# Weaving the mixers of the first half: other step counts behind the matmuls of a hybrid decoder trunk

## The chip, the cores and the metric

The kernel runs on one core of a Trainium2 chip. The metric is device time in microseconds (us). A chip run is repeated, and one execution is taken with the hardware profiler on.

## The reference

Two layers work on x of 1024 rows (tokens) by 1024 columns, in float32. Each layer normalises its input and projects it into three groups of mixers, whose outputs are joined and projected back; then follows a gated MLP with a short causal convolution.

```python
proj = rms_norm(x) @ w_in[layer]
dq, dk, dv, lq, lk, lv, z, xbc, dt = jnp.split(proj, IN_OFFSETS, axis=-1)
o_diff = diff_attention(rope(dq), rope(dk), dv, ...)      # 4 heads, two softmaxes each, causal
o_dil = dilated_attention(rope(lq), rope(lk), lv)         # 6 heads, three sliding windows merged
o_ssd = ssd_mixer(z, xbc, dt, conv_w, ...)                # conv, silu, scan over chunks of 128
x = x + rms_norm(concat(o_diff, o_dil, o_ssd) @ w_out[layer])
g, val = jnp.split(causal_dwconv(rms_norm(x) @ ffn_up[layer]), 2, axis=-1)
x = x + rms_norm((silu(g) * val) @ ffn_down[layer])
```

## The kernel before

Each layer is worked off in two halves T = 0 and 1 of 512 tokens. A product in float32 is made of three matmuls of rounded parts: high by high, high by low and low by high. ScalarE rounds a weight tile (line 144), VectorE subtracts to get the low part (line 145); there are four tiles of each part and three raw ones.

The program is one long list, written out by Python generators, of dense units (matmuls of the projections) and mixer steps. A scheduler of the framework turns the list into one fixed order for every engine, each queue in order. `weave(dense, mixer, counts)` (line 229) takes one dense unit after another, and behind each hangs as many mixer steps as `counts` says. `marks` holds certain matmuls of the unit, every sixth in a block of 24. Step x of n is written with high priority, and its TensorE instructions are ordered behind mark (x + 1) * len(marks) // n - 1, counted from 0. The gate holds TensorE alone; the step's work on other engines is free to go as its data come.

In a layer's first half the order is this. The unit kinds are: six rotary units of dilated heads (`DILC`), four of differential heads (`DIFC`), and seven convolution units (`SSDC`). An `mm3` block (line 216) is 24 matmuls of 512 columns for one half. `DILC` runs alone for T = 0. The first weave has `DIFC` for T = 0 (one block a unit) and `SSDC` for both halves (two blocks a unit). The second weave has `DILC` and `DIFC` for T = 1 (ten units of a block) and four units of the token-major projection `tm_in(1)`, of 24 matmuls of 384 columns each. The third weave has the first three output units `out_units(0)`. After it the rest of both is run out, and the MLP follows, with the heads of T = 1 woven into it.

The mixer list of T = 0 is: 30 steps of three pairs of dilated heads, 22 of two pairs of differential heads, one step that loads five finished head tiles and splits them (`out_load`, line 778), 16 of four state-space chunks: 69. A head pair has eight softmax steps (four blocks of queries, two heads). In `attn` (line 657) step z makes scores (line 610) and softmax (612 to 615; 733 to 735 for the differential pairs, 727 and 728 for the dilated ones) of item z, transposes item z - 1 (750, 751), and multiplies item z - 2 with the values (760). Six steps at the end of each generator drain it; some of them do nothing. `load_head` (line 618) brings queries and keys of the next pair in when the present one is in its last block of queries; of query tiles there are four, which two differential heads fill.

In `ssd` (line 480) a chunk has three steps. The first transposes and scales the inputs and makes the decay matrix (lines 520 to 544); VectorE multiplies it at line 546. The second adds the carried state's part (555 to 560). The third first calls `finish` (line 489, transposes at 492) for the chunk before, then multiplies (566), sums and gates (568, 569), updates the state (572 to 580), and normalises (585, `rstd` at 108 with POOL's power at 114, 589). One step stands ahead of the first chunk, three behind the last, of which the third is its `finish`.

A convolution block is evacuated by `conv` (line 370) with three long VectorE instructions at line 374, then a tanh and a product (391, 392), into scratch tiles of the tag cv, of which there are four, and written to DRAM (393). A rotary block takes two or four products (402, 403, 408 to 411), two roundings (415) and two subtractions on POOL (417). PSUM holds three accumulators. All DMAs are issued by the one queue of SP.

Of the kernel before, what the change touches and what calls it, by code (L numbers as in the profile page):

```python
# [69 lines left out]
def body(ctx, tc, x_in, win, wva, wvb, wvz, wout, wup, wdn, cst, gains, dtb, alog, lamp, kst, rope, out):  # L70
# [158 lines left out]
    def weave(dense, mixer, counts):  # L229
        for n in counts:  # L230
            marks.clear()
            next(dense, None)
            for x in range(n):
                gate = marks[(x + 1) * len(marks) // n - 1]
                with tc.high_priority(), tc.issue_after(gate.ins):
                    next(mixer, None)

    def act_pair():
        return (sp.tile([P, KT, H], F32R, tag="act", bufs=4, name="ah"),
                sp.tile([P, KT, H], F32R, tag="act", bufs=4, name="al"))  # L240
# [68 lines left out]
    def run(*gens):  # L309
        for g in gens:  # L310
            for _ in g:
                pass

    for l in range(NL):
# [113 lines left out]
        def in_unit(name, Ts):  # L428
            hi, lo = wsplit(win[l, IN_IDX[name]])
            for T in Ts:  # L430
                a = acc()
                mm3(a, hi, lo, rhs_of(hT[T]), KT)
                in_evac(name, T, a)
# [38 lines left out]
        def dt_steps(T):  # L472
            dt_chain(T)
            yield
            dt_sums(T)
            yield
# [301 lines left out]
        def out_load(T, pair, ks):  # L778
            for k in ks:
                m = t2("cv", 4)  # L780
                Y.dma_start(m[:], MT[k][T][:] if k < 5 else MS[T][:, k - 5])
                out_split(pair, k, m[:])
            yield

        def tm_in(T, before=None):
            def evac(c, t, a):
                v = t2("cv", 4)
                c0, n = ((0, 384), (384, 256), (640, 384))[c]
                v, a, d = v[:, :n], a[:, :n], a[:, n:n + 6]
                if c < 2:  # L790
                    A.activation(v, a, AF.Copy)
                else:
                    A.activation(v, a, AF.Tanh, scale=0.5)
                    V.scalar_tensor_tensor(v, v, 1.0, a, op0=ALU.add, op1=ALU.mult)
                Y.dma_start(VZ[T][t, :, c0:c0 + n], v)
                if c == 1:
                    e = slice(t * 6, t * 6 + 6)
                    V.tensor_tensor(dtr[T][:, e], d, sm[:, e], op=ALU.add)
                    if t == 3 and T == 0:
                        dt_chain(0)  # L800
            return tm_units([wva[l], wvb[l], wvz[l]], 0, KT, rhs_of(hT[T]), evac, before, pairs=0 if before else 1)

        def out_units(T, pair):
            xs = []
            g1 = load_gain(l, 1)
            g2 = load_gain(l, 2)
            rr = [None] * 4
            sq = [None] * 4

            def evac(c, t, a):  # L810
                if c == 0:
                    rr[t] = rows()
                    sq[t] = tiny()
                A.activation(rr[t][:, c * H:(c + 1) * H], a[:], AF.Copy)
                A.activation(a[:], a[:], AF.Square, accum_out=sq[t][:, c:c + 1])
                if c == 0 and t == 3:
                    xs.extend(load_x(T))
                if c == 1:
                    V.tensor_tensor(sq[t][:, 0:1], sq[t][:, 0:1], sq[t][:, 1:2], op=ALU.add)
                    norm_add(4 * T + t, xs[t], rr[t][:], sq[t], rr[t], g1, False, g2)  # L820
            return tm_units([wout[l, c] for c in range(2)], 0, KT, rhs_of(pair), evac, pairs=1 if T else 0), rr
# [27 lines left out]
        def down_group(T, gi, fT):  # L849
            k0, n = GROUPS[gi]  # L850
            last = gi == len(GROUPS) - 1
            f = [fT[:, 2 * t:2 * t + 2].rearrange("p k n -> p (k n)") for t in range(4)]
            if last and T:
                xs = load_x(T)
                g3 = load_gain(l, 3)
                g0 = load_gain(l + 1, 0) if l < NL - 1 else None

            def evac(c, t, a):
                d = slice(c * H, (c + 1) * H)
                if gi == 0:  # L860
                    A.activation(f[t][:, d], a[:], AF.Copy)
                else:
                    V.tensor_tensor(f[t][:, d], a[:], f[t][:, d], op=ALU.add)  # L863
                if last and T and l == NL - 1:
                    if c == 0:
                        fin.append((rows(), tiny()))
                    r, sq = fin[-1]
                    A.activation(r[:, d], f[t][:, d], AF.Square, accum_out=sq[:, c:c + 1])
                    if c == 1:
                        V.tensor_tensor(sq[:, 0:1], sq[:, 0:1], sq[:, 1:2], op=ALU.add)  # L870
                        rs = rstd(sq[:, 0:1], 1, 1.0 / DM, EPS)
                        for d in (slice(0, H), slice(H, DM)):
                            V.scalar_tensor_tensor(r[:, d], f[t][:, d], rs[:, 0:1], g3[:, d], op0=ALU.mult, op1=ALU.mult)
                            E = G if d.start == 0 else V
                            E.tensor_tensor(r[:, d], xs[t][:, d], r[:, d], op=ALU.add)
                            Y.dma_start(out[4 * T + t, :, d], r[:, d])
                elif last and T and c == 1:
                    fin.append(fin_norm(4 * T + t, xs[t], f[t], g3, g0))
            return tm_units([wdn[l, c] for c in range(2)], k0, n, [gt[k0 + k] for k in range(n)], evac, inner=last and T == 1)
# [18 lines left out]
        def ffn(T, pair, fT):  # L898
            for gi, (k0, n) in enumerate(GROUPS):
                for j in range(k0, k0 + n):  # L900
                    yield from up_pair(T, j, pair)
                if gi < len(GROUPS) - 2:
                    yield from down_group(T, gi, fT)

        SSDC = IN_ORDER[:7]
        DILC = IN_ORDER[7:13]
        DIFC = IN_ORDER[13:]

        def units(names, Ts):
            for n in names:  # L910
                in_unit(n, Ts)
                yield

        NG = len(GROUPS)
        if l == 0:
# [16 lines left out]
            dense = tm_in(0, before)  # L932
# [18 lines left out]
        else:  # L951
            cs, sw, fw, sm, nA, nlam = layer_constants()
            hT[0] = nextT
            dense = tm_in(0)
# [2 lines left out]
        dt_sums(0)  # L957
        run(units(DILC, (0,)))
        mix0 = chain(attn(0, DILH), attn(0, DIFH))
        weave(chain(units(DIFC, (0,)), units(SSDC, (0, 1))), mix0, [2] * 4 + [4] * 7)  # L960
        pair = act_pair()
        mix0 = chain(mix0, out_load(0, pair, range(5)), ssd(0, pair))
        tm1 = tm_in(1)
        weave(chain(units(DILC + DIFC, (1,)), tm1), mix0, [2] * 14)
        mix1 = chain(attn(1, DILH + DIFH), dt_steps(1), ssd(1))
        dense, rs = out_units(0, pair)
        weave(dense, mix0, [3] * 3)
        run(mix0)
        run(dense)
        hold[0] = lastmm[0]  # L970
# [18 lines left out]
        dense, rs = out_units(1, pair)  # L989
        run(dense)  # L990
        hold[0] = lastmm[0]
        dense = down_group(0, NG - 1, fT0)
# [4 lines left out]
        dense = ffn(1, hp, fT1)  # L997
# [8 lines left out]
        dense = down_group(1, NG - 2, fT1)  # L1006
# [89 lines left out]
```

## Time and profile before

| what | us |
|---|---|
| median of 3 runs | 2672.4 (2667.95 to 2674.1) |
| the profiled execution's own time | 2669.15 |
| its span, first to last instruction | 2667.4 |
| TensorE busy (matmuls) | 2605.3 |
| TensorE weight loads | 2163.8 |
| VectorE busy | 1832.6 |
| ScalarE busy | 1247.7 |
| GpSimd (POOL) busy | 230.3 |
| mean granted TensorE clock | 0.995 |

PE is TensorE's matmuls, PEld its weight loads, DVE VectorE, ACT ScalarE, POOL GpSimd, SP the queue that issues DMAs. Busy time is the union of an engine's instructions. An arrow in brackets behind an instruction says how long its engine had been idle before it and what ended that. The clock is granted at 2.4 GHz (1.00) or 1.2 GHz (0.50).

### The profile page before, as it was taken

Reading aid. Unit: us, or ns where it says so; the run is one execution under the profiler, and the core shown is the slowest. Engines: PE = TensorE matmul, PEld = TensorE weight load, DVE = VectorE, ACT = ScalarE, POOL = GpSimd, SP = SyncE. Lnnn points to the kernel's source line nnn. Section 1 sums busy time; section 2 is a strip of 40 time slices with the busy share of each in tenths; the row PEclk is TensorE's granted clock in tenths of the full one; section 3 lists DMA queues with packets and bytes.
Section 4 is the critical chain, followed back from the end, with each engine's and each line's share of the span. In section 5 each row is a group of like instructions: output and inputs, shape, how many; then the busy total and the mean of one; then the engine's idle time right before and its main releaser. Section 6 shows DMA issues by size and latency. Waiting matters only on the chain.

```text
span 2667.4 us, 37072 instructions
## 1 busy us (share of the span) xinstructions
PE 2605.3 (98%) x13448; PEld 2163.8 (81%) x13448; DVE 1832.6 (69%) x3854; ACT 1247.7 (47%) x2179; POOL 230.3 (9%) x228
## 2 busy tenths in 40 slices
PE   7999999999999999999999999999999999999998
PEld 6887788888788877888888878788877888788886
DVE  5567856567877586666765688565688775956666
ACT  4465444555544454333444654455565344543332
POOL 0100210110002010000002012101100110100001
PEclk9999999999999999999999999999999999999999
DMA  6654635344434454333347546454444334633332
GB/s 227 202 185 146 206 121 186 111 119 115 123 101 128 125 187 155 97 95 95 91 161 232 167 142 203 139 161 115 121 115 139 94 111 133 231 97 95 95 99 67
DMA packets 163718, 368.90 MB, mean 138 GB/s; under 512 B 18256, under 2 KB 64208, under 8 KB 163536
## 3 DMA queue, kind: packets, MB, share of 16 engines
q1 hardware_dynamic: 163536, 366.54, 44.1%
q8 instruction: 106, 1.74, 0.3%
q14 instruction: 76, 0.62, 0.1%
HBM read 306.18 MB, written 60.29 MB: 137 GB/s over the span
## 4 chain that ended last, share of the span: by engine, by line
PE 81%; DVE 9%; ACT 3%; DMA 3%; issue 3%; POOL 1%; SPq 0%; ACTq 0%; DVEq 0%; POOLq 0%
PE acc L220 16%; PE acc L223 15%; PE acc L224 15%; PE acc L168 7%; PE acc L164 7%; PE acc L167 7%; PE po L760 4%; PE s L610 3%; PE tr L750 3%; DVE wl L145 1%; POOL rs_r L114 1%; ACT wh L144 1%; DVE P L287 1%; DVE t L288 1%; DMA cv<-MT 1%
## 5 line engine op out<-in xcount | busy, mean ns | idle before, releaser
L220 PE MATMUL acc<-ah,wh 128*128 128x512 f32 x1952 | 775.4, 398 | 0.5 <-ACT ah L271 0.5
L224 PE MATMUL acc<-ah,wl 128*128 128x512 f32 x1952 | 764.8, 392 | 0.0
L223 PE MATMUL acc<-al,wh 128*128 128x512 f32 x1952 | 764.4, 392 | 0.2 <-DVE al L272 0.2
L145 DVE TENSOR_TENSOR wl<-wr,wh 128x1024 fp32r<-128x1024 f32 (+3 forms) x406 | 477.9, 1183 | 274.9 <-ACT wh L144 271.1
L144 ACT ACTIVATE wh<-wr 128x1024 fp32r<-128x1024 f32 (+3 forms) x406 | 406.2, 1007 | 470.0 <-PE acc L223 269.1
L220 PEld LDWEIGHTS acc<-ah,wh 128*128 128x128 f32 x1952 | 366.6, 188 | 80.5 <-issue 9.3
L224 PEld LDWEIGHTS acc<-ah,wl 128*128 128x128 f32 x1952 | 366.6, 188 | 78.1 <-issue 2.4
L223 PEld LDWEIGHTS acc<-al,wh 128*128 128x128 f32 x1952 | 366.9, 188 | 71.7 <-DVE al L272 1.0
L374 DVE SCALAR_TENSOR_TENSOR cv<-acc,cs,cv 128x511 f32<-128x511 f32 (+2 forms) x436 | 324.6, 744 | 17.7 <-ACT cv L372 15.8
L164 PE MATMUL acc<-wh,g 128*128 128x512 f32 x704 | 281.0, 400 | 4.5 <-DVE fT L863 2.2
L167 PE MATMUL acc<-wl,g 128*128 128x512 f32 x704 | 276.5, 393 | 3.0 <-DVE wl L145 3.0
L168 PE MATMUL acc<-wh,g 128*128 128x512 f32 x704 | 275.8, 394 | 0.9 <-DVE g L843 0.9
L164 PE MATMUL acc<-wh,ah 128*128 128x512 f32 (+2 forms) x640 | 225.4, 356 | 10.0 <-ACT wh L144 6.7
L167 PE MATMUL acc<-wl,ah 128*128 128x512 f32 (+2 forms) x640 | 226.3, 354 | 5.8 <-DVE wl L145 5.1
L168 PE MATMUL acc<-wh,al 128*128 128x512 f32 (+2 forms) x640 | 225.1, 353 | 4.3 <-DVE al L272 4.1
L615 ACT ACTIVATE P<-P,tiny 128x128 f32<-128x128 f32 (+7 forms) x224 | 172.9, 773 | 115.1 <-DVE tiny L614 110.4
L612 DVE CUSTOM_DVE_ANT_0 P<-s,kc 128x512 f32<-128x512 f32 (+3 forms) x224 | 129.7, 588 | 108.6 <-PE s L610 107.2
L114 POOL TENSOR_TENSOR rs_r<-rs_m,kc 128x1 f32<-128x1 f32 (+2 forms) x88 | 71.4, 815 | 1398.4 <-DVE rs L115 1256.6
L164 PEld LDWEIGHTS acc<-wh,g 128*128 128x128 f32 x704 | 132.8, 189 | 39.2 <-ACT g L842 3.8
L372 ACT ACTIVATE cv<-acc,cs 128x512 f32<-128x512 f32 x204 | 155.7, 763 | 13.8 <-PE acc L224 13.3
L168 PEld LDWEIGHTS acc<-wh,g 128*128 128x128 f32 x704 | 132.6, 188 | 31.9 <-DVE g L843 4.4
L167 PEld LDWEIGHTS acc<-wl,g 128*128 128x128 f32 x704 | 133.0, 189 | 29.6 <-DVE wl L145 3.8
(173 smaller groups left out, 3138.2 us busy)
## 6 DMA issues: line engine op xcount, KB each, us to landing
wr<-in_wup SPq DMA_DIRECT2D x176, 512.0 KB, 3.6
wr<-in_wdn SPq DMA_DIRECT2D x80, 512.0 KB, 3.5
wr<-in_win SPq DMA_DIRECT2D x54, 512.0 KB, 5.1
wr<-in_wout SPq DMA_DIRECT2D x32, 512.0 KB, 4.4
xd<-t SPq DMA_DIRECT2D x24, 512.0 KB, 2.9
t<-xd SPq DMA_DIRECT2D x24, 512.0 KB, 3.7
t<-in_x SPq DMA_DIRECT2D x16, 512.0 KB, 4.7
Q<-DQ SPq DMA_DIRECT2D x128, 64.0 KB, 2.1
```

What stands on the lines that cost most here:

```text
L144: A.activation(h, r, AF.Copy)
L145: V.tensor_tensor(part(lo), r, fr(h), op=ALU.subtract)
L164: i = T_.matmul(a, xh, hi[:, w], start=(n0 + k == 0), stop=False)
L167: T_.matmul(a, xh, lo[:, w], start=False, stop=False)
L168: lastmm[0] = T_.matmul(a, xl, hi[:, w], start=False, stop=(n0 + k == n - 1))
L220: i = T_.matmul(a[:], hi[:, w], xh, start=(k == 0), stop=False)
L223: T_.matmul(a[:], hi[:, w], xl, start=False, stop=False)
L224: i = T_.matmul(a[:], lo[:, w], xh, start=False, stop=(k == nk - 1))
L372: A.activation(u[:], a[:], AF.Identity, scale=w[:, n:n + 1], bias=w[:, taps:taps + 1])
L374: V.scalar_tensor_tensor(u[:, d:], a[:, :H - d], w[:, n - d:n - d + 1], u[:, d:], op0=ALU.mult, op1=ALU.add)
L612: V.tensor_tensor_reduce(p[:, c:c + n], s[:, :n], mask[:, o:o + n], 1.0, -1e30 if c == 0 else mx[:, e], ALU.add, ALU.max, mx[:, e])
L615: A.activation(p[:, :nk * P], p[:, :nk * P], AF.Exp, scale=scale, bias=nm[:, e], accum_out=den[:, e])
```

## The change

Three lists of counts are changed, the same way in both layers. The number of mixer steps, their content and their order among themselves stay.

```diff
-        weave(chain(units(DIFC, (0,)), units(SSDC, (0, 1))), mix0, [2] * 4 + [4] * 7)
+        weave(chain(units(DIFC, (0,)), units(SSDC, (0, 1))), mix0, [3] * 4 + [5] * 7)
         pair = act_pair()
         mix0 = chain(mix0, out_load(0, pair, range(5)), ssd(0, pair))
         tm1 = tm_in(1)
-        weave(chain(units(DILC + DIFC, (1,)), tm1), mix0, [2] * 14)
+        weave(chain(units(DILC + DIFC, (1,)), tm1), mix0, [2] * 5 + [1] * 9)
         mix1 = chain(attn(1, DILH + DIFH), dt_steps(1), ssd(1))
         dense, rs = out_units(0, pair)
-        weave(dense, mix0, [3] * 3)
+        weave(dense, mix0, [2] * 3)
```

## Rows read from the trace of the kernel before

**Rows 1.** The page: busy time by engine, and the chain that ended last.
```profile
PE 2605.3 (98%) x13448; PEld 2163.8 (81%) x13448; DVE 1832.6 (69%) x3854; ACT 1247.7 (47%) x2179; POOL 230.3 (9%) x228
...
PE 81%; DVE 9%; ACT 3%; DMA 3%; issue 3%; POOL 1%; SPq 0%; ACTq 0%; DVEq 0%; POOLq 0%
```

**Rows 2.** Busy time by stretch, layer 0: stretch, length, each engine (instructions), clock, DMA.
```profile
core 0: us, PE busy (x) PEld busy (x) DVE busy (x) ACT busy (x) POOL busy (x), PEclk, DMA share, GB/s
76.29:109.04 32.75, 32.75 (x146) 27.12 (x146) 17.07 (x22) 8.94 (x12) 5.48 (x4) 1.00 0.72 238
109.04:237.00 127.96, 127.51 (x691) 103.14 (x689) 85.75 (x247) 76.29 (x168) 8.29 (x6) 1.00 0.56 173
237.00:311.50 74.50, 74.41 (x393) 58.37 (x392) 62.10 (x168) 39.05 (x86) 15.39 (x11) 1.00 0.60 194
311.50:346.00 34.50, 31.75 (x189) 29.93 (x188) 29.24 (x51) 15.02 (x39) 11.82 (x11) 0.95 0.52 166
346.00:372.00 26.00, 24.59 (x123) 19.77 (x122) 10.27 (x29) 11.91 (x33) 5.00 (x5) 1.00 0.40 136
```

**Rows 3.** Busy time by stretch, the chunks of layer 1.
```profile
1632.00:1666.00 34.00, 32.08 (x192) 30.45 (x190) 29.09 (x51) 15.08 (x38) 12.07 (x11) 0.95 0.55 174
1666.00:1692.00 26.00, 24.55 (x123) 19.80 (x122) 10.77 (x29) 11.99 (x34) 5.00 (x5) 1.00 0.42 141
```

**Rows 4.** Instructions in order of time, TensorE, 300 to 345: start, us, what.
```profile
314.54 1.55 PE L566 MATMUL tr<-xdt,P 128*128 128x64 f32 x12 [0.68 <-DVE P L546]
...
327.39 0.78 PE L492 MATMUL tr<-kc,yq 128*128 128x128 f32 x3 [1.51 <-ACT yq L589]
...
332.66 0.53 PE L164 MATMUL acc<-wh,ah 128*128 128x384 f32 x1
...
333.76 0.33 PE L167 MATMUL acc<-wl,ah 128*128 128x384 f32 x1
```

**Rows 5.** Instructions in order of time, TensorE, 345 to 380.
```profile
361.10 0.33 PE L492 MATMUL tr<-kc,yq 128*128 128x128 f32 x1 [0.89 <-ACT yq L589]
```

**Rows 6.** Lines 568 and 589, 300 to 372: duration ns min/median/max, first and last start.
```profile
L568 DVE TENSOR_TENSOR y<-tr,y x4: 541/550/557, 317.3 to 355.0; 128x384 f32<-128x384 f32 x4
...
L589 ACT ACTIVATE yq<-y,rs_r x8: 438/454/465, 326.9 to 361.0; 128x192 f32<-128x192 f32 x8
```

**Rows 7.** Busy time 198.21 to 311.50, VectorE, lines 612, 614, 733, 734, 735 singly.
```profile
198.21:311.50 113.29, 14.80 (x64) 1.00 0.54 171
...
198.21:311.50 113.29, 4.64 (x33) 1.00 0.54 171
...
198.21:311.50 113.29, 2.51 (x16) 1.00 0.54 171
...
198.21:311.50 113.29, 3.42 (x16) 1.00 0.54 171
...
198.21:311.50 113.29, 8.65 (x16) 1.00 0.54 171
```

**Rows 8.** Busy time by stretch, the fifth and the seventh convolution unit of layer 0.
```profile
198.21:211.01 12.80, 12.80 (x70) 10.29 (x69) 6.89 (x15) 4.78 (x10) 0.00 (x0) 1.00 0.61 170
222.97:237.00 14.03, 14.03 (x74) 11.19 (x74) 12.96 (x51) 9.07 (x27) 0.00 (x0) 1.00 0.25 78
```

**Rows 9.** Instructions in order of time, TensorE, 216 to 223: a head's scores, its transpose.
```profile
219.18 0.33 PE L610 MATMUL s<-k,Q 128*128 128x128 f32 x2
...
222.91 0.30 PE L750 MATMUL tr<-kc,P 128*128 128x128 f32 x1 [0.45 <-DVE P L735]
```

**Rows 10.** Instructions in order of time, SP's DMA issues, 180 to 262.
```profile
241.52 8.70 SPq L646 DMA_DIRECT2D Q<-DQ  x15
```

**Rows 11.** Instructions in order of time, POOL (268 to 300), then VectorE (270 to 281).
```profile
272.80 3.73 POOL L417 TENSOR_TENSOR g<-g 128x512 fp32r<-128x512 f32 x2 [8.03 <-issue]
...
273.13 2.24 DVE L145 TENSOR_TENSOR wl<-wr,wh 128x1024 fp32r<-128x1024 f32 x1
...
276.76 1.21 DVE L145 TENSOR_TENSOR wl<-wr,wh 128x1024 fp32r<-128x1024 f32 x1
```

**Rows 12.** Busy time of one stretch in the MLP of layer 0.
```profile
992.00:1024.00 32.00, 31.96 (x142) 26.12 (x140) 30.21 (x60) 17.89 (x26) 2.61 (x4) 1.00 0.53 167
```

## The prediction

> **What bounds the kernel now.** I read the page's first section before anything else: TensorE has a matmul in flight for 98% of the span, and the chain of work that ended last runs through it for 81% [rows 1]. So only two things can shorten the program: TensorE idle time inside the changed stages, and time in which its clock was granted at half rate. The second view is busy time by stretch. Of layer 0 it shows the six undisturbed blocks of 24 matmuls ahead of the weave (32.75 us, so 5.46 us a block), the first weave (109.04 to 237.00), ten rotary units (to 311.50), and the two stretches in which the state-space chunks run (311.50 to 346.00 and 346.00 to 372.00) [rows 2]. The reader is to see that the first weave and the rotary units lose 0.45 and 0.09 us, while the chunks lose 2.75 and 1.41 us and have a mean granted clock of 0.95 in the former stretch. Layer 1 repeats it: 1.92 and 1.45 us idle, clock 0.95 [rows 3]. The third view, the matmuls in order of time, names the waits: the diagonal product (line 566) waits 0.68 us for VectorE's line 546, and the transposes of a normalised chunk (line 492) 1.51 us for ScalarE's line 589; soon after, a 384-column matmul takes 0.53 us where 0.33 is usual, which is the granted clock at 1.2 instead of 2.4 GHz [rows 4]; line 492 waits again, 0.89 us, in the output units [rows 5].
>
> **What the change removes.** No instruction is added or removed, DMAs included: the same 69 mixer steps (52 of the heads, one that loads finished heads, 16 of the chunks) are hung behind other matmuls. Before, the first weave takes 8 + 28 = 36 steps, the second 28, the third the last 5. After, they take 12 + 35 = 47, then 10 + 9 = 19, then 3. So eleven head steps move from the rotary units up into the convolution units, and the chunks start five units earlier, in the fourth unit of the second weave (key rotary) instead of the ninth, and from the sixth unit on have one step a unit.
>
> Before, in chunk 0 line 568 starts at 317.3 us and ScalarE's first line 589 only at 326.9: 9.6 us from sum to normalised chunk, in a stretch where VectorE is busy 29.24 of 34.50 us; the last chunk takes 6.0 us, 355.0 to 361.0, up to the last of its two instructions [rows 2, 6]. Steps at two a unit come back to `finish` about three steps later, one and a half units. With one step a unit, three whole units lie between, three times four to five and a half microseconds: 9.6 us is covered. The last chunk's third step stands behind the last unit of the second weave, and its `finish` in the middle of the second output unit: one and a half blocks, 8.2 us, against 6.0. What is late next there is nothing of the chunk: line 546 and the state update have a unit to themselves.
>
> So I price the gain as all idle time of the four chunk stretches and both clock drops. Idle: 2.75 + 1.41 + 1.92 + 1.45 = 7.5 us [rows 2, 3]. Clock: 5% of 34.5 and of 34.0 us, 1.7 us each, 3.4 us; the drop follows the longest wait in layer 0 and layer 1 has the same mean, so I let it go with that wait. Sum 10.9 us. Its lower end is the case where only the wait of 1.51 us, taken once a layer, and the clock drops go, 6.4 us; above it I count nothing, since the stages behind have their own waits.
>
> **What it costs.** The eleven head steps now lie beside convolution, where VectorE is the helper in demand. The sixteen softmax steps of the differential heads cost VectorE 14.80 + 4.64 + 2.51 + 3.42 + 8.65 = 34.0 us by line, 2.13 us each [rows 7]. A convolution unit of two blocks takes 6.89 us of VectorE with no softmax beside it, and 1.21 us for the weight split that this stretch doesn't contain: 8.1 us [rows 8, 11]. The last three such units get, at five steps, the second to sixteenth step of the differential heads, fourteen softmax steps of VectorE: 3 x 8.1 + 14 x 2.13 = 54.1 us. TensorE needs 32.75 us for their six blocks and about 1.2 us a step: up to 311.50 it is busy 127.51 + 74.41 = 201.9 us, less 28 blocks (152.8), over some 40 working steps; 15 steps make 18, together 50.7 us. VectorE is asked for 3.4 us more than TensorE takes; the finishing of a pair of heads, which I don't price, comes on top. Before, the seventh unit with four steps had VectorE at 12.96 of 14.03 us and lost nothing [rows 8].
>
> What covers 3.4 us: three accumulators, so evacuation may lag two blocks (10.9 us); four weight tiles, so splits run units ahead; and a second weave whose first three units hold almost no softmax. A stretch elsewhere, 32 us at 30.21 us of VectorE, lost 0.04 us of TensorE [rows 12]. So I take the overload at nothing, and if the cover were gone it costs 3.4 us a layer or, with the pair's finishing, about twice that (an estimate).
>
> Second cost: a head step's transposes (line 750) need its softmax (scores, maximum, exponential, sum, scaling). From scores to transposes passed 3.73 us in the step at 219.18, of which TensorE stood 0.45 us [rows 9]. Gates were twelve matmuls apart (2.73 us by the block of 24); of three or five steps a unit two gaps are six matmuls, 1.36 us: two in each of four and seven units, 22 in all. Each could wait as that one did; or nothing, as the steps fall behind their gates and matmuls of the dense unit go first, which 35 of the 36 steps of before did. I take three new waits of 0.45 us a layer, 2.7 us for both, nearest to that row; the ends are 0 and 22 x 0.45 x 2 = 19.8 us.
>
> Third, the queue of loads on SP. Heads of the second differential pair are fetched by 16 query loads, of which fifteen in a row held the queue for 8.70 us among rotary units [rows 10]. They now stand among convolution units, whose writes of finished channels queue behind and keep their scratch tiles. Cost 0 while evacuation lags by less than two blocks, 8.7 us a layer if not covered at all; I take 0, since 8.7 is under 10.9. The part of POOL and ScalarE is the same work beside other units, and the third weave's smaller count keeps `finish` at the same matmul; both cost nothing as long as TensorE has units to run.
>
> Sum: -10.9 + 2.7 = **-8.2 us**. On the profiled execution's own 2669.15 us (span 2667.4 and 1.75 around it) that is 2661.0. It lies 3.25 us under the median of the runs, 2672.4; on the median the forecast is **2664.2 us**.
>
> **A rule that speaks against it.** Two POOL subtractions took 3.73 us in a row where VectorE's weight split, begun beside them, took 2.24 us, against 1.21 for the next one [rows 11]: 1.03 us lost. The Trainium skill (SBUF — State Buffer, section "Who interferes with whom") says why: a VectorE instruction with two SBUF inputs and a GpSimd instruction that reads SBUF share a read interface, and one blocks while the other runs. The trace agrees by that pair. By the rule the chunks, whose products have two such inputs, are slowed by the ten subtractions of the rotary units in the second weave; this is the third rival below.
>
> **Rivals.** *First, the heads wait for their own softmax.* Half of the 22 tight gaps wait 0.45 us: 9.9 us for both layers, net -1.0, 2671.4. For it speaks that the one wait of before is of this kind; against it, that it is one in 36, though gaps of 2.73 us were already shorter than the 3.73 us of the chain.
>
> *Second, the other side: convolution's evacuation becomes the bound.* Head steps go ahead of dense work on VectorE, so in the last three convolution units the 3.4 us (or twice that) fall on evacuation, and the load burst holds the scratch tiles at the same place. It decides from the point where evacuation lags more than two blocks, 10.9 us: then all three accumulators are full and TensorE stops. Both fully exposed are 3.4 + 8.7 = 12.1 us a layer; I set three quarters, 9.1 us, so 18.2 - 10.9 = +7.3: 2679.7, slower. For it: VectorE at 92% in that stage already [rows 8]. Against it: the stretch of [rows 12], and that the steps' lag hands the work on to units with room.
>
> *Third, the backlog doesn't drain.* Ten collisions of 1.03 us take 10.3 us of VectorE's room in the second weave, so the overload of 3.4 us meets the chunks and comes back there as their old kind of wait, while the tight gaps take 2.7: -10.9 + 2.7 + 6.8 = -1.4, 2671.0.
>
> *Fourth, the change doesn't do what it says:* the chunks' waits come from late loads and not from the spacing, and only the last two, 1.41 and 1.45 us, go: -2.9, 2669.5.
>
> **How the numbers follow.** Forecast 0.57; first rival 0.15; second 0.15; third 0.06; fourth 0.07. A change of 0.2%, 5.3 us, is about what can be told from none here. Faster by more: the forecast, 0.57. Within: first, third and fourth rival, 0.28. Slower by more: the second, 0.15. The range goes from 2657 (all waits gone, nothing new, and some 4 us by which runs differ) to 2677, short of the second rival's time but past its smaller half; the forecast's own is 2660 to 2668.
>
> **What would show it.** Right: in the stretch after the rotary units no wait of lines 492, 555 and 566 over 0.3 us and a granted clock of 1.00 in both layers; about 4 us less idle a layer there; the chunks' first matmuls beside rotary units; at most four waits of line 750 a layer. Wrong: TensorE waiting in the last three convolution units for an accumulator or for a split (the second rival); many waits of line 750 under half a microsecond (the first); line 492 still waiting for line 589 (third or fourth); or a new stall of the clock elsewhere.

## The result, and the profile after

| | before | after |
|---|---|---|
| median, us | 2672.01 (2667.95 to 2674.1, 6 runs) | 2687.28 (2684.16 to 2691.44, 6 runs) |
| profiled execution, own time | 2669.15 | 2684.53 |
| its span | 2667.4 | 2682.7 |

The ratio is 1.0058, 95% interval 1.0047 to 1.0069: slower by 0.6%, where 0.3% faster was forecast. The page of the profile says at once that no matmul was added (13448 in both): of the 15.3 us of span TensorE has 6.9 us more in flight (part of it at half rate), the rest is standing [rows 1].

```profile
PE 2612.2 (97%) x13448; PEld 2166.4 (81%) x13448; DVE 1839.6 (69%) x3854; ACT 1246.5 (46%) x2179; POOL 235.9 (9%) x228
```

Busy time by stretch, with the columns of [rows 2]: the first weave, the ten rotary units, the token-major projection, and the output units with what is run out behind them. First layer 0, then the first two of layer 1.

```profile
109.42:253.06 143.64, 142.21 (x772) 110.23 (x771) 99.63 (x324) 87.53 (x209) 9.67 (x7) 1.00 0.54 162
253.06:335.09 82.03, 75.56 (x381) 62.21 (x379) 69.99 (x129) 34.82 (x69) 23.53 (x18) 0.96 0.56 185
335.09:358.23 23.14, 23.14 (x150) 22.92 (x148) 16.09 (x26) 11.12 (x24) 9.32 (x7) 1.00 0.70 219
358.23:404.23 46.00, 45.79 (x210) 37.65 (x209) 20.11 (x44) 19.88 (x45) 2.92 (x5) 1.00 0.37 114
...
1437.68:1581.46 143.78, 142.09 (x772) 110.42 (x771) 99.64 (x324) 87.48 (x209) 10.03 (x7) 1.00 0.53 162
1581.46:1662.79 81.33, 75.66 (x381) 62.22 (x379) 70.09 (x129) 34.83 (x69) 23.60 (x18) 0.96 0.57 187
```

The reader is to see two opposite things. The third and fourth stretch, where the chunks used to stall, have 0.00 and 0.21 us of idle time and the full clock. But the rotary units, which lost 0.09 us [rows 2], now lose 6.47 us, have a clock of 0.96, and the first weave loses 1.43 us instead of 0.45. The four stretches together went from 288.8 to 294.8 us in layer 0, from 287.6 to 294.3 in layer 1: 12.7 of the 15.3 us. (Of the rest, 1.4 us is one more stretch at half clock behind the chunks of layer 1.)

TensorE's waits in 109 to 405 us, by what ended them (total us, times, longest):

```profile
PE tr L572 <- DVE y L568: 4.9, 1, 4.9
PE tr L699 <- DVE on L694: 1.5, 1, 1.5
PE po L760 <- DMA vv<-VZ: 0.8, 1, 0.8
PE tr L750 <- DVE P L735: 0.5, 1, 0.5
```

One wait is most of it, and the line named, VectorE's 568, isn't its cause. VectorE's queue is in order, so the question is what stood ahead of line 568. In order of time, after; first SP, then ScalarE, POOL, VectorE, TensorE:

```profile
289.08 1.74 SPq L781 DMA_DIRECT2D cv<-MT  x4
...
307.72 6.05 SPq L426 DMA_DIRECT2D MX<-g  x4
313.82 0.90 SPq L364 DMA_DIRECT2D g<-in_rope  x1
314.78 0.45 SPq L365 DMA_DIRECT2D g<-in_rope  x1
...
307.06 0.63 ACT L415 ACTIVATE g<-g 128x512 fp32r<-128x512 f32 x1 [3.54 <-DVE g L410]
...
309.29 1.99 POOL L560 TENSOR_TENSOR y<-y,ys 128x384 f32<-128x384 f32 x1
311.24 1.98 POOL L417 TENSOR_TENSOR g<-g 128x512 fp32r<-128x512 f32 x1
...
304.29 0.95 DVE L509 TENSOR_TENSOR P<-kc,dtv 128x768 fp32r<-128x768 f32 x1
305.15 0.68 DVE L409 TENSOR_TENSOR g<-acc,g 128x512 f32<-128x512 f32 x1
...
306.35 0.68 DVE L410 TENSOR_TENSOR g<-g 128x512 f32<-128x512 f32 x1
...
308.56 3.54 DVE L145 TENSOR_TENSOR wl<-wr,wh 128x1024 fp32r<-128x1024 f32 x2
317.90 0.69 DVE L402 TENSOR_TENSOR g<-acc,g 128x512 f32<-128x512 f32 x1 [5.80 <-DMA g<-in_rope]
...
319.62 0.55 DVE L568 TENSOR_TENSOR y<-tr,y 128x384 f32<-128x384 f32 x1
...
314.91 0.39 PE L223 MATMUL acc<-al,wh 128*128 128x512 f32 x1
320.22 1.65 PE L572 MATMUL tr<-xdt,Q 128*128 128x192 f32 x4 [4.93 <-DVE y L568]
...
323.37 0.63 PE L220 MATMUL acc<-ah,wh 128*128 128x512 f32 x1
```

Read backwards: TensorE waits for line 568, which stands behind line 402. Line 402 is the first product of the first differential rotary unit, and waited 5.80 us for its rope tables. The tables' loads (364, 365) were issued at 313.8 and 314.8 because ahead of them on SP stood the four writes of the rotary block before (426), which held the queue from 307.72. The last of these needed POOL's second subtraction, done at 313.2, behind the chunk's line 560 on POOL and behind ScalarE's rounding, which itself waited for VectorE's line 410 at 306.35. Line 410 was late in VectorE's own queue: between lines 408 (300.55) and 409 of the same rotary block stood the products of a chunk's first step, lines 522 to 509, up to 305.24. Before, the same writes held the queue for 2.57 us, and the finished heads' loads (781) came behind the tables:

```profile
290.76 2.57 SPq L426 DMA_DIRECT2D MX<-g  x4
293.67 0.53 SPq L364 DMA_DIRECT2D g<-in_rope  x1
...
295.87 0.42 SPq L781 DMA_DIRECT2D cv<-MT  x1
```

Back to the kernel after: from 319.3 us on, still inside the wait, the clock is granted at half rate for 6.8 us; TensorE is busy for 5.9 of them (0.63 us a matmul of 512 columns where 0.39 is usual): 3.0 us more.

### The profile page after: what moved, and what is told of

Same layout as the page of the kernel before. It is cut to its first block, busy times and chain, and to the rows that moved or that the text cites. A ratio compares the mean times of both kernels' runs of the same rounds, so it can differ in the third digit from the quotient of the medians.

```text
span 2682.7 us, 37051 instructions
## 1 busy us (share of the span) xinstructions
PE 2612.2 (97%) x13448; PEld 2166.4 (81%) x13448; DVE 1839.6 (69%) x3854; ACT 1246.5 (46%) x2179; POOL 235.9 (9%) x228
## 4 chain that ended last, share of the span: by engine, by line
PE 80%; DVE 9%; issue 3%; ACT 3%; DMA 3%; POOL 2%; SPq 0%; ACTq 0%; POOLq 0%; DVEq 0%
PE acc L220 15%; PE acc L223 15%; PE acc L224 15%; PE acc L168 7%; PE acc L164 7%; PE acc L167 7%; PE po L760 4%; PE s L610 3%; PE tr L750 3%; DVE wl L145 2%; POOL rs_r L114 1%; ACT wh L144 1%; DVE cv L374 1%; DVE P L287 1%; DVE t L288 1%
```

## The experiments

Times are medians of 5 to 12 executions; the ratio is to the kernel before, run beside it (2672.2 to 2673.3 us). "Busy" is TensorE's busy time in the four stretches of one layer less what half clock took of it (half of the time that TensorE was busy at half clock): 281.6 to 282.1 us before, 283.7 after.

**Tables loaded ahead.** The changed kernel, with the tables loaded ahead of the second weave, into a gain tile that is idle there:

```diff
+        tg = sp.tile([P, DM], F32, tag="gb", bufs=2, name="tg")
+        Y.dma_start(tg[:, :H], rope[0, :, H:2 * H])
+        Y.dma_start(tg[:, H:], rope[1, :, H:2 * H])
+        ropeT[(0, 1)] = tg[:, :H], tg[:, H:]
         weave(chain(units(DILC + DIFC, (1,)), tm1), mix0, [2] * 5 + [1] * 9)
```

> The changed kernel, but the two rotary tables of the differential heads of T = 1 are loaded ahead of the second weave into a gain tile that is idle there, instead of behind the writes of the mixed rotary tiles on SP's queue. Theory A (late tables): in the changed kernel VectorE stands 5.8 us at line 402 for those tables, with the chunk's line 568 queued behind it, and TensorE's line 572 waits 4.9 and 4.1 us and then runs 6.8 us at half clock in each layer. Then these waits fall under 0.5 us, the half clock goes (3.4 us a layer), and the time falls by 14 to 16 us to 2670 to 2674. Rival B (contention): the chunks' own work is too slow beside rotary units, since VectorE and POOL are in each other's way there; the tables only happen to be what VectorE stood at. Then line 572 or 492 still waits 3 us or more a layer and the time stays above 2680.

2682.83 us, 1.0041 (1.0026 to 1.0055). Theory A mostly missed; its rival's time came, above 2680 us, but not its waits of 3 us or more. In layer 0 the wait for line 568 shrank to 2.3 us in two parts and the half clock in the rotary units went, but a wait of 2.0 us for line 403 came at the next place. The tables are one link of the chain, not its beginning.

**The heads alone.** The changed kernel's first weave; the chunks at two steps a unit, from the ninth unit, as before:

```diff
-        weave(chain(units(DILC + DIFC, (1,)), tm1), mix0, [2] * 5 + [1] * 9)
+        weave(chain(units(DILC + DIFC, (1,)), tm1), mix0, [1] * 5 + [0] * 3 + [2] * 6)
...
-        weave(dense, mix0, [2] * 3)
+        weave(dense, mix0, [3] * 3)
```

> Only the first half of the change: first weave at three and five head steps a unit, chunks at the units and at two steps a unit as before (second weave 1 x5, 0 x3, 2 x6, third 3 x3). Theory A: the denser first weave costs about 1 us of TensorE a layer (the wait for the values tile at line 760 and little else), so the time is that of before, +0 to +4 us, and lines 492 and 566 wait as before. Rival C (overload, the second rival of the prediction): VectorE's surplus in the last three convolution units is what costs; then +8 us or more, with TensorE waiting for accumulators there.

2686.96 us, 1.0058 (1.0045 to 1.0071): as slow as the whole change, with no chunk beside the rotary units up to there. Theory A missed; rival C's 8 us or more came, but not its mechanism, as no wait of the first weave is for an accumulator. So a loss of this size needs no chunk products on VectorE and POOL. The same place fails, along another way (ScalarE, VectorE, TensorE, in order of time):

```profile
295.46 0.72 ACT L775 ACTIVATE ah<-cv,cs 128x512 fp32r<-128x512 f32 x1 [6.75 <-DMA cv<-MT]
...
301.16 1.94 ACT L775 ACTIVATE ah<-cv,cs 128x512 fp32r<-128x512 f32 x3
303.00 0.62 ACT L415 ACTIVATE g<-g 128x512 fp32r<-128x512 f32 x1
...
310.87 0.69 DVE L402 TENSOR_TENSOR g<-acc,g 128x512 f32<-128x512 f32 x1 [4.40 <-DMA g<-in_rope]
...
313.17 0.77 PE L220 MATMUL acc<-ah,wh 128*128 128x512 f32 x1 [3.70 <-DVE g L403]
```

ScalarE's queue holds the splits of the finished heads (line 775) ahead of the rotary rounding (415), and the first split waits 6.75 us for its load.

**The chunks' spacing alone.** The first weave as before; the heads' last 16 steps in the first four rotary units:

```diff
-        weave(chain(units(DIFC, (0,)), units(SSDC, (0, 1))), mix0, [3] * 4 + [5] * 7)
+        weave(chain(units(DIFC, (0,)), units(SSDC, (0, 1))), mix0, [2] * 4 + [4] * 7)
...
-        weave(chain(units(DILC + DIFC, (1,)), tm1), mix0, [2] * 5 + [1] * 9)
+        weave(chain(units(DILC + DIFC, (1,)), tm1), mix0, [4] * 4 + [2] + [1] * 9)
```

> Only the other half: first weave as before, heads at four a unit in the first four rotary units, then chunks at one step a unit from the fifth unit on (second weave 4 x4, 2, 1 x9; third 2 x3 with the last chunk in it). Theory A: the chunk's work lies beside the mixed rotary units again, so the tables come late again: VectorE stands 2 us or more at line 402 for the table's DMA, and a chunk line of TensorE waits for it; time +3 to +12 us over before. Rival C: the first weave being as before, nothing is lost; the time is before's or 5 to 10 us better.

2664.11 us, 0.9971 (0.9960 to 0.9982): faster than both kernels. Theory A missed again; rival C's 5 to 10 us better came. Busy time by stretch:

```profile
109.37:237.39 128.02, 127.57 (x692) 103.17 (x690) 85.66 (x247) 76.32 (x168) 8.28 (x6) 1.00 0.56 173
237.39:319.20 81.81, 79.52 (x426) 62.51 (x425) 72.05 (x183) 42.45 (x95) 20.50 (x14) 1.00 0.58 191
319.20:342.96 23.76, 23.44 (x149) 22.86 (x149) 18.60 (x33) 12.12 (x26) 8.82 (x7) 1.00 0.63 203
342.96:394.00 51.04, 50.63 (x245) 42.15 (x245) 27.73 (x60) 23.28 (x57) 6.28 (x9) 1.00 0.39 122
```

Here VectorE is busier in the rotary units than in the changed kernel (72.05 of 81.81 us, against 69.99 of 82.03), and TensorE loses 2.29 us there at full clock. The chunks' waits in the last two stretches are gone as in the changed kernel.

**Tables ahead, nothing else.** The kernel before with the four lines of the first experiment:

> The kernel before with the same early tables as in the first experiment, as its control. Theory A: before, VectorE stood about 2 us at line 402 and TensorE didn't notice; so the time is that of before within 3 us. If early tables are worth something for another reason, it is 5 us or more faster, and the gain of the first experiment has to be read against this kernel.

2669.28 us, 0.9991 (0.9982 to 0.9999): no difference that counts. Where the tables aren't late, loading them ahead buys next to nothing.

**The finished heads' load later.** The changed kernel, with that one step moved seven chunk steps back:

```diff
-from itertools import chain
+from itertools import chain, islice
...
-        mix0 = chain(mix0, out_load(0, pair, range(5)), ssd(0, pair))
+        s0 = ssd(0, pair)
+        mix0 = chain(mix0, islice(s0, 7), out_load(0, pair, range(5)), s0)
```

> Changed kernel, with the one step that loads the finished heads hung seven chunk steps later, so that its loads no longer stand beside the chunk steps of the fourth and fifth rotary unit. Theory D (the loss beside the rotary units is one chain: finished heads' loads and chunk products delay the scalar and POOL part of a rotary unit, its write waits at the head of SP's queue, the rope tables come late, VectorE's line 402 waits for them in order, TensorE behind it; the rest of the loss is some 3 us a layer of mixing in the first weave): the wait of TensorE at line 572 (4.9 and 4.1 us) falls below 1.5 us and the half clock behind it goes, 2674 to 2680 us. Rival E (the place of the loads is of no matter, the chunk products alone make the delay): the wait stays, 2685 to 2689.

2675.25 us, 1.0004 (0.9993 to 1.0016). 12 us come back by moving five loads and their ten split instructions; the seven chunk steps ahead of them stand one place earlier for it, and the run doesn't tell the two apart. The wait for line 568 is

```profile
PE tr L572 <- DVE y L568: 1.0, 1, 1.0
```

and the clock is 1.00 in all eight stretches. Theory D held, rival E didn't. On VectorE the second chunk's products were done by 299.52 us, ahead of lines 408 and 409 (300.71 and 301.31), and line 410 came 3.4 us sooner, though TensorE ended that block 0.7 us later (300.7 against 300.0):

```profile
302.98 0.68 DVE L410 TENSOR_TENSOR g<-g 128x512 f32<-128x512 f32 x1
```

**Heads early, chunks spaced as in the faster variant.**

```diff
-        weave(chain(units(DILC + DIFC, (1,)), tm1), mix0, [2] * 5 + [1] * 9)
+        weave(chain(units(DILC + DIFC, (1,)), tm1), mix0, [2, 2, 1, 0, 2] + [1] * 9)
```

> Heads as early as in the changed kernel (three and five steps a unit), chunks at the places of the variant with the chunks' spacing alone, which ran in 2664.1 us; from that one it differs in the first weave and in the count of head steps left to the first rotary units. Theory D (mixing costs 3 us a layer and about 1 us of idle in the first weave, and early heads move the finished heads' loads up): 2671 to 2686. Rival F (only the chunks' earlier start costs; the heads' earlier place is free, and the variant with the heads alone lost by its empty units): 2662 to 2667.

2678.98 us, 1.0028 (1.0018 to 1.0038). Against the variant with the spacing alone only head steps differ, and it is 15 us slower: rival F fell.

**Four steps earlier, and seven.** Both have the faster variant's chunk places (second weave `[3] * 4 + [2] + [1] * 9`, and `[3] * 3 + [0, 2] + [1] * 9`); the first weave is

```diff
-  [3] * 4 + [5] * 7
+  [3] * 4 + [4] * 7
...
-  [3] * 4 + [5] * 7
+  [2] * 4 + [5] * 7
```

> As the variant with the chunks' spacing alone, but three instead of two head steps in each of the first weave's four earlier units (four steps earlier, the seven later units keep four each). Theory D (what costs is the breaking up of runs of the product with values, at five steps a unit above all): 2664 to 2668. Rival G (each step moved up costs alike, a third of the loss for four of eleven): 2668 to 2672.

> As the variant with the chunks' spacing alone, but five instead of four head steps in each of the first weave's seven later units (seven steps earlier). Theory D: runs of the product with values are cut where gates stand six matmuls apart, some 2 us a layer, and VectorE's convolution work is late: 2668 to 2676. Rival F (the heads' place is free): 2662 to 2667.

2685.36 us, 1.0049 (1.0034 to 1.0063), and 2675.07 us, 1.0008 (0.9999 to 1.0017). Four steps cost 21 us, seven 11, eleven 15: nothing like a price per step. Both theories missed with four steps; with seven, theory D's range held. The waits with four steps say why: it is again the tables' place (line 402 waited 4.21 us for them), then half clock. SP in the variant with four steps:

```profile
297.32 1.74 SPq L781 DMA_DIRECT2D cv<-MT  x4
...
306.03 6.42 SPq L426 DMA_DIRECT2D MX<-g  x4
312.50 0.58 SPq L364 DMA_DIRECT2D g<-in_rope  x1
```

and in the one with the spacing alone, whose heads finish later, so that the tables go ahead of the finished heads' loads:

```profile
293.59 3.78 SPq L426 DMA_DIRECT2D MX<-g  x4
297.43 0.57 SPq L364 DMA_DIRECT2D g<-in_rope  x1
...
299.50 0.42 SPq L781 DMA_DIRECT2D cv<-MT  x1
```

With four steps the loads had left the queue at 299.06. It isn't they that hold it at 306, but the writes, which wait for the rotary unit's own chain.

**Load later and tables ahead, together**, in the changed kernel:

> Changed kernel with the finished heads' load seven chunk steps later (2675.3 us alone) and the rope tables of the second family loaded ahead of the second weave (2682.8 alone). Theory D (what the later load repairs is the late tables, what is left is 3.2 us a layer of TensorE's own work from cut runs, 1.5 us at line 699, small waits): the tables add next to nothing, 2670 to 2676. Rival E (tables and loads are two losses that add up): about 2671 or less, down to 2667.

2670.68 us, 0.9994 (0.9985 to 1.0004). It lies in both ranges, so it doesn't tell the theories apart. Its busy time is 284.1 us in layer 0, its idle time in the four stretches 4.1.

**Tables ahead in the variant with four steps.**

> The variant with four head steps earlier (2685.4 us), with the tables loaded ahead. Theory D (its loss is the wait of 4.1 us a layer at line 164 behind VectorE's line 402, which waits for the tables, and the half clock after it, 1.7 us a layer): 2673 to 2677. Rival H (the tables are only where lateness shows, and the rotary units' write would be late all the same): 2681 to 2687.

2674.12 us, 1.0008 (0.9999 to 1.0017): 11 us back, as theory D had it; rival H fell. TensorE's longest wait in the four stretches of layer 0 without and with the tables ahead:

```profile
PE acc L164 <- DVE g L403: 4.1, 1, 4.1
```

```profile
PE tr L699 <- DVE on L694: 3.2, 1, 3.2
```

The second was there without the tables ahead too (3.3 us): transposes that wait for the last heads' normalising (line 694). Why that is late isn't shown.

**Eight steps earlier, no unit of five.** First weave `[4] * 4 + [4] * 7`, second `[2] * 4 + [2] + [1] * 9`, the third as in the changed kernel.

> Chunks as in the variant with their spacing alone, eight head steps earlier, but all of them in the four units of the first kind: four steps in each of the eleven units, none of five. TensorE's busy time at full clock in the four stretches of a layer was 281.1 us with the heads as before, 282.1 with seven steps moved to units of five, 284.3 with eleven. If cut runs make it, 281.1 to 282.0 here; if every moved step costs (0.29 us each), 283.4. Whole time: 2664 to 2668 with no wait for tables, 2672 to 2685 with one.

2683.74 us, 1.0051 (1.0039 to 1.0063), with waits for the tables again (1.6 and 2.0 us at line 164). Its busy time was 284.1 us in layer 1 (the row sums the four stretches; the clock is 1.00 in each):

```profile
sum 292.18, PE 284.10 PEld 231.40 DVE 206.22 ACT 152.38 POOL 46.45; mean PE 71.02 PEld 57.85 DVE 51.56 ACT 38.10 POOL 11.61
```

That is not the 281.1 to 282.0 that I expected of units without five steps; the rival's 283.4 is nearer. But the products with values (line 760) stood in 30 separate runs a layer here, as in the changed kernel, where they have 23 before, 24 with the spacing alone, 25 with four steps earlier, 26 with seven. The busy times go with these counts, roughly (281.8, 281.2, 282.2, 282.0; with 30 runs 283.4 to 285.3), and not with five a unit.

**The spacing alone, with the tables ahead.**

> The variant with the chunks' spacing alone (2664.1 us), with the tables loaded ahead. Theory D: its line 402 waits only 0.7 us for them, hidden, so the same, 2661 to 2666. Rival: the table tiles' release from the shared tag lets other rotary work go sooner and saves a part of the small waits: 2657 to 2661.

2665.08 us, 0.9972 (0.9962 to 0.9982), the same as without, as theory D had it.

**Runs cut, no step moved.** The faster variant, with the second part of a product tied behind the unit's next mark:

```diff
-    marks = []
+    marks, nextm = [], [None]
...
-                gate = marks[(x + 1) * len(marks) // n - 1]
+                gate, nextm[0] = (marks + [None])[(x + 1) * len(marks) // n - 1:][:2]
...
-                            T_.matmul(st["po"][g * 64:(g + 1) * 64, i * P:(i + 1) * P], st["v"][:, b, g * 64:(g + 1) * 64],
-                                      pt[:, g, b * P:(b + 1) * P], start=(b == 0), stop=(b == nk - 1))
+                            mo = T_.matmul(st["po"][g * 64:(g + 1) * 64, i * P:(i + 1) * P], st["v"][:, b, g * 64:(g + 1) * 64],
+                                      pt[:, g, b * P:(b + 1) * P], start=(b == 0), stop=(b == nk - 1)); T == 0 and b and b == nk // 2 and g == 0 and nextm[0] and queue_behind(mo, nextm[0])
```

> The variant with the chunks' spacing alone (2664.1 us); no step is moved, but in the weaves of the first half the second part of a product with values (line 760) is tied behind the next mark of the dense unit, which gives six more runs of such matmuls a layer (24 to 30, as many as in the changed kernel); VectorE, ScalarE and POOL keep their order. Theory D2 (the 2 to 3 us a layer that TensorE's own work grew by with the heads earlier are cut runs): busy time at full clock in the four stretches of a layer goes from 281.2 to 283.5 to 284.3 us, the whole to 2668 to 2671 us. Rival I (the growth belongs to the steps moved, whatever their runs): 281.2 to 281.7 us a layer, 2662 to 2666 in all.

2670.24 us, 0.9990 (0.9981 to 0.9999), 6 us more than without (the two profiled executions lie 4.2 us apart, and busy time alone makes 4.3). Sums of the four stretches of layer 0, the variant with the spacing alone, then the cut one:

```profile
sum 284.63, PE 281.15 PEld 230.68 DVE 204.04 ACT 154.16 POOL 43.88; mean PE 70.29 PEld 57.67 DVE 51.01 ACT 38.54 POOL 10.97
```

```profile
sum 286.77, PE 283.36 PEld 230.17 DVE 204.21 ACT 154.29 POOL 43.89; mean PE 70.84 PEld 57.54 DVE 51.05 ACT 38.57 POOL 10.97
```

Idle time is the same (3.48 and 3.41 us), busy time 2.2 us more for six cuts, 0.37 us a cut: a little under the 2.3 to 3.1 of theory D2, far above rival I. One product of 16 matmuls, TensorE in order of time, uncut and then cut:

```profile
175.26 1.09 PE L760 MATMUL po<-pt,vv 128*64 128x128 f32 x16
176.28 0.50 PE L220 MATMUL acc<-ah,wh 128*128 128x512 f32 x1
176.62 0.39 PE L223 MATMUL acc<-al,wh 128*128 128x512 f32 x1
```

```profile
176.17 0.66 PE L760 MATMUL po<-pt,vv 128*64 128x128 f32 x8
176.76 0.50 PE L220 MATMUL acc<-ah,wh 128*128 128x512 f32 x1
...
178.02 0.40 PE L224 MATMUL acc<-ah,wl 128*128 128x512 f32 x1
178.35 0.66 PE L760 MATMUL po<-pt,vv 128*64 128x128 f32 x8
178.93 0.50 PE L220 MATMUL acc<-ah,wh 128*128 128x512 f32 x1
```

From start to start the whole run takes 1.02 us, the halves 0.59 and 0.58, and each passage between kinds some 0.1 us more (0.33 or 0.34 instead of 0.23 from a matmul of 512 columns to what follows): 0.15 + 0.1 + 0.1 for a cut.

## Why the prediction was wrong, point by point

**The removal was right.** "All idle time of the four chunk stretches and both clock drops", 10.9 us: measured 11.1 (idle 4.3 in layer 0, 3.4 in layer 1, twice 1.7 of clock). Lines 492, 555 and 566 have no wait over 0.3 us there, and the variant with the spacing alone, which keeps this part and leaves the heads, came out at 2664.1 us. That the forecast had 2664.2 is chance: it holds 2.7 us for waits of line 750, and this variant loses 2.3 us in the rotary units of layer 0 instead.

**The step that failed** is the third cost's last sentence: "The part of POOL and ScalarE is the same work beside other units [...] both cost nothing as long as TensorE has units to run." The work is the same, but its chain has a length, and the head steps that were moved away had been its cover. What came is the last of the prediction's own signs of being wrong, "a new stall of the clock elsewhere". A rotary block is multiplied (VectorE), rounded (ScalarE), subtracted twice (POOL) and written (SP); only then are tables of the next kind loaded, for which VectorE's in-order queue stops. The table takes, of layer 0, the time at which TensorE goes on to the block after the first differential one (first matmul of line 220), the time of the first one's line 402, and the wait of TensorE that follows it:

| kernel | TensorE goes on | line 402 | behind by, us | wait, us |
|---|---|---|---|---|
| before | 293.1 | 298.1 | 5.0 | none |
| spacing alone | 295.4 | 301.4 | 6.0 | 0.3 |
| load later | 307.9 | 315.8 | 7.9 | 1.0 |
| both spaced | 301.5 | 312.1 | 10.7 | 2.0 |
| seven early | 304.1 | 316.2 | 12.0 | 1.7 |
| after | 306.0 | 317.9 | 11.9 | 4.9 |
| heads alone | 298.4 | 310.9 | 12.4 | 3.7 |
| four early | 302.5 | 316.5 | 14.0 | 4.1 |

In these rows a lag of up to 6 us is covered, and one of about 8 or more isn't; layer 1 divides them the same way. The lag doesn't give the length of the wait (11.9 and 12.0 us stand beside 4.9 and 1.7), and with the tables ahead in the changed kernel line 402 came only 4.9 us behind and TensorE still waited 1.0 us for line 568.

Two things lengthen the lag. Units empty of heads pass in 5.5 us (28.4 to 50.6 us from the start of the rotary units, four units, in the heads-alone kernel), so TensorE comes sooner. And heads that end earlier bring the finished heads' loads and splits beside the rotary block whose writes the tables stand behind: in the heads-alone kernel the splits hold ScalarE ahead of its rounding, in the changed kernel the chunk products that come behind them hold VectorE ahead of its line 409. Counted from the start of the rotary units (237.0 us before, 253.1 after, 253.3 with the heads alone), TensorE came to the block 3.1 us sooner in the changed kernel (52.9 against 56.1) and line 402 3.7 us later (64.8 against 61.1); in the heads-alone kernel TensorE came 10.9 us sooner and line 402 3.5. That the place of the load step decides in the changed kernel the later load shows (12 us back), and that the tables are where it shows, the four-step pair (11 us back). By which of its parts (the splits gone, the chunk's products sooner) the later load helps isn't settled, and the tables ahead gave only 4.5 us in the changed kernel alone.

**What it added up to**, both layers, the four stretches: new idle time 14.1 us (9.0 at line 572, 3.0 at line 699, 1.8 at line 760, the rest small), half clock in the rotary units 6.0, busy time 3.7; less 11.1; +12.7.

**Busy time wasn't priced at all.** I said that no instruction is added, and took TensorE's own time as fixed. Its order was not: steps set closer cut the products into 30 runs instead of 23. At 0.37 us a cut, seven are 2.6 us a layer; measured 1.7 and 2.0 in the changed kernel, 2.2 and 2.7 with the load later, whose four stretches are at full clock. What makes the kernels with 30 runs differ among themselves (283.4 to 285.3 us) is open.

**First cost, VectorE's overload at nothing: right in the first weave.** No accumulator and no weight split stops TensorE there; the second rival named the right sign for a mechanism that didn't happen; its price, +7.3, was half of what came. The finishing of a pair of heads, which was left unpriced, is what line 699 waits for in the rotary units: 1.5 us a layer.

**Second cost, three new waits of line 750, 2.7 us:** two waits a layer instead of one (0.5 and 0.2 us), 0.4 in all. The first rival fell.

**Third cost, the load queue at 0:** line 760 waits 0.8 and 1.0 us a layer for its values' load; small, but most of the first weave's 1.1 us more of idle time.

**The third rival's collision** is seen: POOL's 560 and 417 took 1.99 and 1.98 us while VectorE's two splits of line 145 took 3.54, which alone take 1.21 each [rows 11]. By the rule of the Trainium skill (SBUF — State Buffer, section "Who interferes with whom") a VectorE instruction with two SBUF inputs and a GpSimd instruction that reads SBUF hold each other up on a shared read interface; the trace agrees by about 1.1 us of VectorE. It stands in the chain above, but in the heads-alone kernel POOL's two subtractions of that chain took 1.29 and 1.35 us (1.50 and 1.98 after) and the stall came all the same, so it isn't needed for it. What it adds after no run takes apart. The fourth rival fell with the removal.

## What to carry to other kernels

A step taken out from beside a dense unit takes away the time that the unit's own evacuation had: before moving it, follow the unit's chain through every in-order queue to the next thing that needs its tiles, and compare its length with the shorter unit. Order of issue is a cost as well: look at which loads a shared queue meets first once a producer ends earlier, and count how many separate runs the small matmuls fall into. When a change has two halves, price and time them apart; here one was worth 8 us, and the other cost 15 by itself and 23 on top of it.

## What the runs showed of the hardware that I had not expected

- Breaking a run of the small matmuls of line 760 (128*64 weights, 128 columns) between matmuls of 512 columns costs 0.37 us a cut (2.2 us for six), without any wait: 0.15 us in the run itself, about 0.1 at each passage.
- With a single wait of 4.9 us came 6.8 us at half clock, begun 0.9 us before the wait's end, 3.0 us lost; in the variant with the load later, waits of 1.5 and 1.0 us in the same stretches were followed by none, whereas before one of 1.51 us was [rows 4]. At line 699 a wait of 3.26 us came with 3.4 us at half clock in the variant with four steps (from 291.4, the wait ended at 291.9), one of 3.24 us with the tables ahead came with none.
- The loss is not gradual: with the same chunk places, 4, 7, 8 and 11 head steps moved gave 21, 11, 20 and 15 us. In all four the first differential block's line 402 waits for its tables; why they come in this order isn't shown.
